# Product operands from host layouts, 1/rms on the results, wider products and some low halves by transfer in a decoder layer

## The chip, the core and the metric

The kernel runs on one core of a Trainium2 chip. The metric is the device time of one execution in microseconds (us). TensorE (PE) multiplies matrices; VectorE (DVE), ScalarE (ACT) and GpSimd (POOL) work on tiles; SyncE (SP) issues the transfers between HBM and the on-chip memory SBUF. Products are summed in PSUM banks of 128 x 512 floats.

## What is computed

The layer takes x of 512 tokens by 1024 features. Everything is float32.

```python
n = rmsnorm(x, norm1_gain)                       # x * rsqrt(mean(x*x) + eps) * gain
q, k, v, u, gates = split(n @ w_in)              # 1024, 1024, 1024, 512, 2048 columns
q, k = rope(rmsnorm(q, q_gain)), rope(rmsnorm(k, k_gain))     # per half head of 64
A = diff_attention(q, k, v, lam)                 # 8 heads, causal; softmax_0 - lam * softmax_1
S = s5_layer(u, ...)                             # a linear recurrence over the tokens, then a GLU
h = x + (sigmoid(g_A) * (A @ w_attn_proj) + sigmoid(g_B) * (S @ w_ssm_proj)) @ w_out
y = h + conv_ffn(rmsnorm(h))                     # w_up, a width-3 causal convolution, a gate, w_down
```

## The kernel before

**Three products for one.** Every float32 operand of a large product is made of a rounded high half and a low half, the rest. `mm3` adds hi·hi, lo·hi and hi·lo into one PSUM bank, so each product of the layer is three matmuls. The activations' halves are `xh`, `xl` (of the normed x, transposed, features on the partitions), `oh`, `ol` (attention), `mh`, `ml` (the mix) and `hh`, `hl` (the second norm).

**Weights.** `load_raw` loads 512 KB into one of 3 buffers `wr`. `split_w` makes the halves: ACT copies `wr` to `wh` (4 buffers, rounded), DVE subtracts to give `wl` (4 buffers). A loaded buffer is free for the next load when both are done.

**Order.** No engine's order is that of the code. The class `Schedule` records every operation with a modelled duration, ranks it by the longest chain behind it plus a number per phase (`sch.boost`), and a list scheduler puts the operations of every engine, SP's transfers too, in a fixed order, within limits on live tiles per class (`sch.caps`). All operations are emitted from one line, L436, so that the profile's groups are told apart by their tiles. The boosts, limits and modelled costs are tables of numbers that decide the order and compute nothing.

**Stages.** (1) The rows of x are loaded; `norm1` squares them on ACT, takes the power -1/2 on POOL (`nrs`), multiplies by 1/rms and gain on DVE (`s_N`), transposes 32 blocks on PE, and writes `xh`, `xl`. (2) q and k of the first head pair (`qk_pair`, by `tok_pair`: 256 columns of weights for two token tiles that share a bank), u (`u_all`, 512 wide, result `Z`), the gates of the S5 branch (`gate_group`, phase `gS`, kept in SBUF), v of the first pair (`v_group`, 256 wide). (3) Four S5 chunks (`s5_const`, `s5_chunk`): constants are built by POOL (`s_T`) and DVE (`k`) from tables of the decay (`dtxe`, `mgxe`), then a scan on DVE with tiles `s_S`; PE transposes and multiplies small float32 blocks between DVE's steps. (4) Projections of the other pairs, the GLU, the S5 projection, eight attention heads, the other gates, the mix, w_out (`tok_pair`, 256 wide), the transposes of `feat`, the second norm, the feed-forward (`ffn`, `down`). Stages overlap: while DVE works on a chunk, PE is given large products.

The widths of a product that the prediction speaks of are the columns that one matmul streams: 256 in `tok_pair`, 512 elsewhere.

Of the kernel before, what the change touches and what calls it, by code (L numbers as in the profile page):

```python
# [15 lines left out]
P = 128  # L16
# [23 lines left out]
C_MASK = 0  # L40
C_DELTA = C_MASK + SEQ
C_COS = C_DELTA + 16
C_SIN = C_COS + NT * HD
C_W = C_SIN + NT * HD

NSLOT = 43


def shape_constants():
    c = np.zeros((P, P + C_W), np.float32)  # L50
    c[:, 0:P] = np.eye(P, dtype=np.float32)
    k = c[:, P:]
    r = np.arange(P)
    k[:, C_MASK + SEQ - P:C_MASK + SEQ] = np.where(r[None, :] <= r[:, None], 0.0, -1e30)
    k[:, C_DELTA:C_DELTA + 16] = (r[:, None] % 16) == np.arange(16)[None, :]
# [3 lines left out]
    cos = np.cos(ang).astype(np.float32)  # L59
    sin = np.sin(ang).astype(np.float32)  # L60
    cc = np.concatenate([cos, cos], -1).reshape(NT, P, HD).transpose(1, 0, 2)
    ss = np.concatenate([-sin, sin], -1).reshape(NT, P, HD).transpose(1, 0, 2)
    k[:, C_COS:C_COS + NT * HD] = cc.reshape(P, -1)
    k[:, C_SIN:C_SIN + NT * HD] = ss.reshape(P, -1)
    return c
# [16 lines left out]
class Op:  # L82
    __slots__ = ("lock", "eng", "calls", "cost", "preds", "succs", "tiles", "alloc", "prio", "npred", "ready", "idx", "start",
                 "end", "nbytes", "phase", "tail", "left", "sim")


class Schedule:
# [4 lines left out]
    DMA_BW = 355.0  # L92
    COLD = 16500.0
# [62 lines left out]
    def _init(self, o, eng):  # L156
        o.eng, o.calls, o.cost, o.preds, o.succs, o.tiles, o.alloc = eng, [], 0.0, {}, [], set(), []
        o.nbytes = 0
        o.lock = False
        o.phase = self.phase  # L160
        o.idx = len(self.ops)
# [102 lines left out]
    def price(self, eng, fn, out, ins, acc, o):  # L264
# [3 lines left out]
        if eng == "PE":  # L268
            if fn == "transpose":
                return 109.0  # L270
            if ins[-1].dtype == F32R:
                c = max(0.4167 * n + 13.5, 98.0 if tuple(ins[0].ap)[-1][0] == 1 else 246.0)

                return c if ins[0].shape[0] > 64 else c / 2
            return 1.667 * n + 11 if out.shape[0] > 32 else 55.0
# [19 lines left out]
        if eng == "POOL":  # L295
            if any(v is ALU.pow for v in [o.calls[-1][2].get("op")]):
# [10 lines left out]
    def rank(self):  # L307
# [3 lines left out]
        for o in reversed(self.ops):  # L311
            dur = o.cost + (1900.0 + o.nbytes / self.DMA_BW if o.eng == "SP" else 0.0)
            o.tail = dur + max([s.tail + self.lat(o, s) for s in o.succs], default=0.0)

    def lat(self, a, b):
        if a.eng == "SP":
            return 0.0
        return self.LAT[a.eng].get(b.eng, 130.0)

    def solve(self):  # L320
# [36 lines left out]
        while done < len(ops):  # L357
# [12 lines left out]
            for e in engs:  # L370
# [31 lines left out]
                o.end = now + cost  # L402
                if e == "SP":
# [35 lines left out]
def build(tc, A, out, dbg=None):  # L439
# [11 lines left out]
    def bc(ap, shape):  # L451
# [9 lines left out]

    sch.caps = {"X": 10, "N": 19, "C": 29, "T": 8, "Z": 15, "S": 18, "G2": 23, "sT": 25, "g": 10, "R": 26,
        "rope": 33, "P": 15, "AT": 15, "O": 8, "pmm": 3, "pa": 2, "px": 1, "po": 1, "p5": 4, "pu": 4, "pq": 9, "pb": 7}

    sch.boost = {"": 6384700, "c0": -125100, "c1": -423900, "c2": 861800, "c3": -573000, "down0": 4913100,
# [5 lines left out]
        "s3": 5910300, "ssm": -676100, "swk": 2750200, "swq": -2342100, "tables": 482600, "u": 1182300,  # L471
# [3 lines left out]
    sch.fifo = set(sch.caps) | {"wr", "wh", "wl", "F", "cv", "h", "mS", "hr"}  # L475
    sch.dram = {"hbuf": {}, "sbuf": {}}
# [117 lines left out]
    vrow = slot("C", [1, 6 * HD])
# [838 lines left out]
```

## Time and profile before

| what | us |
|---|---|
| median of 3 runs | 885.79 (883.72 to 886.74) |
| the profiled execution's own time | 883.83 |
| its span in the trace | 882.1 |
| PE busy | 853.6 (97%) |
| DVE busy | 585.9 (66%) |
| ACT busy | 363.8 (41%) |
| POOL busy | 181.9 (21%) |

The engines work side by side and wait for each other by semaphores. A stretch of the span has a busy time for each engine, and PE a mean granted clock as a share of 2.4 GHz; 0.5 is the lower level of 1.2 GHz. Matmuls overlap in the pipe, so a matmul's own duration is longer than the step from one start to the next; the step is what a stream of them costs. "Idle before, releaser" tells for how long an engine waited ahead of an instruction and what ended the wait.

### The profile page before, as it was taken

What the parts mean: (1) busy time and instruction counts of PE and PEld (TensorE: products, weight loads), DVE (VectorE), ACT (ScalarE), POOL (GpSimd) and SP (SyncE); (2) the same over time, 40 slices, a digit from 0 to 9 for tenths busy, and PEclk for the clock granted to TensorE, in tenths of its full rate; (3) what the DMA queues carried; (4) which work ended last, traced back from release to release, by engine and by line L of the source; (5) the groups of instructions that cost most, each with busy time, mean ns of one, the idle gap of its engine ahead of it and who ended that gap; (6) DMA issues with size and microseconds to landing.
All of it is one profiled execution on the core that took longest, in us unless ns stands there. A gap on an engine that the chain in (4) does not pass through costs nothing.

```text
span 882.1 us, 12703 instructions
## 1 busy us (share of the span) xinstructions
PE 853.6 (97%) x4922; PEld 738.9 (84%) x4922; DVE 585.9 (66%) x1129; ACT 363.8 (41%) x703; POOL 181.9 (21%) x169
## 2 busy tenths in 40 slices
PE   5999899989899999999999999999999999999998
PEld 3998679979679989888889988888888888888887
DVE  4668999899995788864444532599877777324322
ACT  5325462643552466654132531464444444213210
POOL 2445686226103304200000000012211111000000
PEclk9999999989999999999999999999999999999999
DMA  9131113113142301228332652433333333322321
GB/s 286 31 117 49 49 48 94 51 49 97 50 137 91 115 17 49 72 71 273 100 100 85 207 171 76 118 95 96 96 96 95 96 98 99 103 69 86 119 84 59
DMA packets 113208, 85.95 MB, mean 97 GB/s; under 512 B 9634, under 2 KB 99322, under 8 KB 113148
## 3 DMA queue, kind: packets, MB, share of 16 engines
q1 hardware_dynamic: 113148, 85.14, 31.6%
q8 instruction: 38, 0.62, 0.3%
q14 instruction: 22, 0.18, 0.1%
HBM read 78.84 MB, written 6.29 MB: 97 GB/s over the span
## 4 chain that ended last, share of the span: by engine, by line
PE 83%; DVE 10%; ACT 3%; issue 2%; DMA 1%; SPq 1%; POOL 0%; DVEq 0%; ACTq 0%
PE pb L436 83%; DVE s_S L436 4%; DVE wl L436 1%; DVE k L436 1%; DVE s_P L436 1%; DMA s_X<-in_x 1%; ACT s_P L436 1%; DMA wr<-in_w_in 1%; DVE s_rope L436 1%; SPq L436 1%; DVE ml L436 1%; ACT s_G L436 0%; ACT k L436 0%; DVE s_G L436 0%; ACT s_g L436 0%
## 5 line engine op out<-in xcount | busy, mean ns | idle before, releaser
L436 ACT CAST wh<-wr 128x1024 fp32r<-128x1024 f32 (+1 forms) x134 | 139.2, 1039 | 330.1 <-PE pb L436 290.6
L436 DVE TENSOR_TENSOR wl<-wr,wh 128x1024 fp32r<-128x1024 f32 (+1 forms) x134 | 172.3, 1290 | 153.0 <-ACT wh L436 152.6
L436 PE MATMUL pb<-hh,wh 128*128 128x512 f32 (+1 forms) x368 | 140.4, 382 | 0.9 <-ACT wh L436 0.9
L436 PE MATMUL pb<-hh,wl 128*128 128x512 f32 (+1 forms) x368 | 139.8, 380 | 0.0
L436 PE MATMUL pb<-hl,wh 128*128 128x512 f32 (+1 forms) x368 | 139.8, 380 | 0.0
L436 PE MATMUL pb<-wh,xh 128*128 128x256 f32 (+1 forms) x416 | 125.7, 302 | 0.0
L436 PE MATMUL pb<-wh,xl 128*128 128x256 f32 (+1 forms) x416 | 122.2, 294 | 0.1
L436 PE MATMUL pb<-wl,xh 128*128 128x256 f32 (+1 forms) x416 | 122.0, 293 | 0.0
L436 POOL TENSOR_TENSOR s_cv<-s_cv,s_cv 128x512 f32<-128x512 f32 x22 | 37.6, 1707 | 263.1 <-DVE s_cv L436 235.9
L436 PEld LDWEIGHTS pb<-wh,xh 128*128 128x128 f32 x416 | 84.3, 203 | 2.9 <-issue 1.0
L436 PEld LDWEIGHTS pb<-wh,xl 128*128 128x128 f32 x416 | 84.3, 203 | 0.7 <-DVE xl L436 0.4
L436 PEld LDWEIGHTS pb<-wl,xh 128*128 128x128 f32 x416 | 84.2, 202 | 0.0
L436 PEld LDWEIGHTS pb<-hh,wh 128*128 128x128 f32 x368 | 69.2, 188 | 14.2 <-ACT wh L436 1.0
L436 PEld LDWEIGHTS pb<-hh,wl 128*128 128x128 f32 x368 | 69.2, 188 | 13.4 <-issue 0.2
L436 PEld LDWEIGHTS pb<-hl,wh 128*128 128x128 f32 x368 | 69.2, 188 | 13.2
L436 PE MATMUL pb<-wh,s_F 128*128 128x512 f32 (+1 forms) x252 | 71.5, 370 | 0.0
L436 DVE SCALAR_TENSOR_TENSOR s_cv<-s_cv,cw,s_cv 128x511 f32<-128x511 f32 (+1 forms) x88 | 67.7, 805 | 0.0
L436 POOL TENSOR_TENSOR s_T<-k 128x256 f32<-128x256 f32 (+1 forms) x48 | 48.8, 1049 | 22.9 <-DVE k L436 22.9
L436 PEld LDWEIGHTS pb<-wh,s_F 128*128 128x128 f32 x252 | 45.4, 188 | 8.6
L436 PE MATMUL pb<-xh,wh 128*128 128x512 f32 x128 | 52.6, 411 | 0.0
L436 ACT ACTIVATE s_P<-s_P,mx,rq 128x128 f32<-128x128 f32 (+3 forms) x64 | 41.3, 649 | 24.1 <-DVE mx L436 24.1
L436 PE MATMUL pb<-xl,wh 128*128 128x512 f32 x128 | 50.1, 392 | 0.0
(207 smaller groups left out, 1632.1 us busy)
## 6 DMA issues: line engine op xcount, KB each, us to landing
wr<-in_w_in SPq DMA_DIRECT2D x44, 512.0 KB
wr<-in_w_up SPq DMA_DIRECT2D x44, 512.0 KB
wr<-in_w_down SPq DMA_DIRECT2D x20, 512.0 KB
wr<-in_w_attn_proj SPq DMA_DIRECT2D x8, 512.0 KB
wr<-in_w_out SPq DMA_DIRECT2D x8, 512.0 KB
s_X<-in_x SPq DMA_DIRECT2D x8, 256.0 KB
wr<-in_w_ssm_proj SPq DMA_DIRECT2D x4, 512.0 KB
sbuf<-s_g SPq DMA_DIRECT2D x8, 256.0 KB
```

The costliest lines, as they stand in the source:

```text
L436: getattr(e, fn)(*a, **k)
```

## The change

**Layouts made by the host.** x is given a second time transposed (`xt`, 128 x 8 x 512), all weights are cut into 132 tiles of 128 x 1024 (`wt`) that are loaded whole, and the small parameters come laid out and replicated (`pa`, `pb`, `pc`, `rope`, `lam`, `bn`). The transposes of parameters and most spreads by PE are gone.

**1/rms on the results.** `xh`, `xl` are made of `xt` times the gain alone, by one ACT and one DVE operation of 128 x 512 for each of 8 blocks. The power of the mean square (`rs1`) and its spread over the partitions (`rms1`, one 512-wide float32 matmul) come later, and every result is multiplied: `Z` by ACT, q and k within their own norm, v in its two halves' operations, the 16 gate blocks by one more DVE operation each (`V.tensor_mul(g, ps, rms1)`).

**The first product** is u, which needs `xt` and `w_in` two blocks at a time (`k_stream`).

**Wider products.** q and k of a pair share a 512-wide product for each token tile (`qk`), v is made for two pairs at once (`v_half`), w_out in two halves of 512. On PE, 1536 matmuls of 256 columns become 768 of 512; the other large products keep their counts. PE's matmuls go from 4806 to 4000 in all.

**Low halves by transfer.** In the phases `gS`, `v0`, `qk0`, `qk1`, 20 weight tiles in all, ACT writes -hi into `wl` and POOL issues a transfer that adds `wr` to it in SBUF. ACT has 20 more operations of 128 x 1024, POOL 20 transfer issues, DVE 20 subtractions fewer.

**Other moves.** Both sets of gates go through HBM (`gbuf`, `abuf`). Eight matmuls of ones open PE's queue. 1/8 of the softmax is in the rope table. `boost`, `caps` and the modelled costs have new numbers.

```diff
+BY_DMA = ("gS", "v0", "qk0", "qk1")
+WARM = 8
...
+    def split_w(raw):
...
         S.copy(hi, raw)
+        if sch.phase in BY_DMA:
+
+            S.mul(lo, raw, -1.0)
+            G.dma_start(lo, raw, accum_op=ALU.add)
+        else:
             V.tensor_sub(lo, raw, hi.bitcast(F32))
...
+    def k_stream(accs, tiles, lhs, order=None):
+
+        n = len(accs)
+        for j, (wh, wl) in enumerate(tiles):
+            last = j == len(tiles) - 1
+            for i, k in [(i, k) for i in range(n) for k in range(2)] if last else [(i, k) for k in range(2) for i in range(n)]:
+                lh, ll = lhs(2 * j + k, i)
+                with sch.group():
+                    mm3(accs[i], lh, ll, wh[:, k, :], wl[:, k, :], j == 0 and k == 0, last and k == 1)
...
+        S.mul(xh[:, k, :], r, g1col[:, k:k + 1])
+        V.scalar_tensor_tensor(xl[:, k, :], r, g1col[:, k:k + 1], xh[:, k, :].bitcast(F32), op0=ALU.mult, op1=ALU.subtract)
...
+    def gates(off, f):
...
             g = slot("g")
-            S.activation(g, ps, AF.Tanh, scale=0.5)
-            res.append(g)
...
+            V.tensor_mul(g, ps, rms1)
+            S.activation(g, g, AF.Tanh, scale=0.5)
+            f(b, g)
...
+        acc = [pbk("pu") for _ in range(NT)]
+        k_stream(acc, load_k("w_in", KB, (QOFF + 256 * g, 256), (KOFF + 256 * g, 256)), x_tok)
...
+    for ch_ in range(2):
+        sch.phase = f"wout{ch_}"
+        acc = [pbk("pu") for _ in range(NT)]
+        k_stream(acc, load_k("w_out", KB, (512 * ch_, 512)), m_tok)
```

**DVE at the start.** `wl` are low halves of weights, `nms` the mean square, `s_N` the normed x, `s_X` rows of x (of `xt` in the changed kernel). DVE's first instructions before:

```order
L436 TENSOR_TENSOR wl_124<-wr_86,wh_123 128x1024
L436 TENSOR_TENSOR wl_126<-wr_87,wh_125 128x1024
L436 TENSOR_SCALAR nms_108<-nss_105 128x1
L436 SCALAR_TENSOR_TENSOR s_N_110<-s_X_82,nrs_109,pb_103 128x512
L436 SCALAR_TENSOR_TENSOR s_N_112<-s_X_83,nrs_109,pb_104 128x512
L436 TENSOR_TENSOR wl_146<-wr_94,wh_145 128x1024
L436 TENSOR_TENSOR xl<-pb_111,xh 128x4x128
L436 TENSOR_TENSOR xl<-pb_113,xh 128x4x128
L436 TENSOR_TENSOR wl_148<-wr_95,wh_147 128x1024
```

and in the changed kernel, where `cpa` holds the gains:

```order
L485 MEMSET ones 128x128
L485 TENSOR_SCALAR cpa<-cpa 128x4
L485 TENSOR_SCALAR cpa<-cpa 128x1
L485 TENSOR_TENSOR wl_85<-wr_83,wh_84 128x1024
L485 TENSOR_TENSOR wl_90<-wr_88,wh_89 128x1024
L485 TENSOR_TENSOR wl_95<-wr_93,wh_94 128x1024
L485 SCALAR_TENSOR_TENSOR xl<-s_X_82,cpa,xh 128x512
L485 SCALAR_TENSOR_TENSOR xl<-s_X_86,cpa,xh 128x512
```

The norm's steps are gone from ahead of the first `xl`, and three weight tiles stand there.

**POOL at the first S5 chunk.** `s_T` are the decay tables that the chunk's matmuls read, `s_rope` is q or k under the rotation, `qrs` and `rq` are norms of q and k. POOL's instructions before, from the last table of the decay (`mgxe`) on:

```order
L436 TENSOR_TENSOR s_rope_196<-s_rope_194,rck 128x512
L436 TENSOR_TENSOR mgxe_167<-ecol,k_161 128x16
L436 TENSOR_TENSOR s_T_288<-k_161 128x256 x2
L436 TENSOR_TENSOR s_T_289<-k_161 128x256 x2
L436 TENSOR_TENSOR s_rope_204<-s_rope_202,rcq 128x512
L436 TENSOR_TENSOR s_T_291<-k_161 128x256 x2
L436 TENSOR_TENSOR s_T_292<-k_161 128x256 x2
L436 TENSOR_TENSOR qrs_211<-qss_209,mhalf 128x8
L436 TENSOR_TENSOR rq_203<-qss_201,mhalf 128x8
L436 TENSOR_TENSOR s_rope_212<-s_rope_210,rck 128x512
L436 TENSOR_SCALAR rq_203<-rq_203 128x8
```

and in the changed kernel, likewise from `mgxe` on:

```order
L485 TENSOR_TENSOR mgxe_149<-ecol,k_144 128x16
L485 DMA wl_161<-wr_159 128x1024
L485 TENSOR_TENSOR rs_123<-nms_124,mhalf 128x4
L485 DMA wl_164<-wr_162 128x1024
L485 DMA wl_167<-wr_165 128x1024
L485 TENSOR_TENSOR s_T_272<-k_144 128x256 x2
L485 TENSOR_TENSOR s_T_273<-k_144 128x256 x2
L485 TENSOR_TENSOR s_T_275<-k_144 128x256
L485 TENSOR_TENSOR s_T_276<-k_144 128x256
L485 TENSOR_TENSOR s_T_275<-k_144 128x256
L485 TENSOR_TENSOR s_T_276<-k_144 128x256
L485 DMA wl_170<-wr_168 128x1024
L485 DMA wl_209<-wr_207 128x1024
```

Transfers of low halves (`DMA wl`) stand between the multiplies of `s_T` where the norms and rotations stood.

**DVE in the second S5 chunk.** DVE's instructions before, around the first steps on that chunk's results (`s_S<-pb`):

```order
L436 TENSOR_TENSOR wl_270<-wr_266,wh_269 128x1024
L436 TENSOR_TENSOR wl_278<-wr_275,wh_277 128x1024
L436 TENSOR_TENSOR s_S_333<-pb_331,k_162 128x512
L436 TENSOR_TENSOR s_S_334<-pb_332,k_162 128x512
L436 TENSOR_TENSOR s_S_335<-pb_332,k_162 128x512
L436 TENSOR_TENSOR s_S_336<-pb_331,k_162 128x512
L436 TENSOR_TENSOR wl_280<-wr_276,wh_279 128x1024
L436 TENSOR_TENSOR s_S_335<-s_S_335,s_S_336 128x512
L436 TENSOR_TENSOR s_S_333<-s_S_333,s_S_334 128x512
L436 SCALAR_TENSOR_TENSOR s_S_336<-s_T_328,s_S_335 128x512
L436 SCALAR_TENSOR_TENSOR s_S_334<-s_T_328,s_S_333 128x512
```

and in the changed kernel in the same chunk:

```order
L485 TENSOR_TENSOR s_S_317<-pb_315,k_145 128x512
L485 TENSOR_TENSOR s_S_318<-pb_316,k_145 128x512
L485 TENSOR_TENSOR s_S_319<-pb_316,k_145 128x512
L485 TENSOR_TENSOR s_S_320<-pb_315,k_145 128x512
L485 TENSOR_TENSOR s_S_317<-s_S_317,s_S_318 128x512
L485 TENSOR_TENSOR s_S_319<-s_S_319,s_S_320 128x512
L485 SCALAR_TENSOR_TENSOR s_S_318<-s_T_312,s_S_317 128x512
L485 SCALAR_TENSOR_TENSOR s_S_320<-s_T_312,s_S_319 128x512
L485 TENSOR_TENSOR s_S_317<-s_S_318,k_145 128x512
L485 TENSOR_SCALAR qrs_181<-qrs_181,rs_123 128x8
L485 TENSOR_TENSOR s_S_318<-s_S_318,k_145 128x512
```

The subtractions of weights are gone from among the chunk's steps. Ahead of the fourth chunk's last transposes DVE has 28 subtractions of weights before and 5 in the changed kernel.

## Rows read from the trace of the kernel before

**Rows 1.** The page: busy time of each engine, and the chain by engine

```profile
PE 853.6 (97%) x4922; PEld 738.9 (84%) x4922; DVE 585.9 (66%) x1129; ACT 363.8 (41%) x703; POOL 181.9 (21%) x169
...
PE 83%; DVE 10%; ACT 3%; issue 2%; DMA 1%; SPq 1%; POOL 0%; DVEq 0%; ACTq 0%
```

**Rows 2.** Stretches: length, busy PE, PEld, DVE, ACT, POOL (count), clock, DMA share, GB/s

```profile
0.00:40.00 40.00, 29.28 (x182) 25.27 (x182) 20.05 (x38) 16.90 (x33) 11.57 (x26) 0.96 0.59 173
40.00:80.00 40.00, 40.00 (x210) 37.99 (x208) 29.31 (x101) 19.05 (x44) 23.29 (x22) 1.00 0.32 93
80.00:240.00 160.00, 146.81 (x1018) 128.91 (x1018) 150.80 (x296) 73.98 (x163) 75.31 (x74) 0.97 0.20 60
240.00:460.00 220.00, 220.00 (x1385) 189.99 (x1383) 147.56 (x394) 102.03 (x252) 33.14 (x26) 1.00 0.33 102
```

**Rows 3.** Two stretches of 20 us in the S5 stage, same columns

```profile
100.00:120.00 20.00, 17.55 (x85) 14.27 (x85) 19.70 (x34) 8.62 (x19) 11.58 (x12) 0.91 0.15 45
...
180.00:200.00 20.00, 18.01 (x139) 17.26 (x140) 17.84 (x32) 9.61 (x19) 2.55 (x2) 0.83 0.17 54
```

**Rows 4.** Stretch of the first 40 us, instructions that touch xh alone, same columns

```profile
0.00:40.00 40.00, 19.87 (x96) 16.71 (x96) 5.33 (x8) 4.42 (x8) 0.96 0.59 173
```

**Rows 5.** Timeline of PE at 20 us: start, length, instruction, idle time before it

```profile
20.46 0.91 PE L436 MATMUL pb<-ident,s_N 128*128 128x128 f32 x4 [4.37 <-DVE s_N L436]
...
21.38 0.41 PE L436 MATMUL pb<-wh,xl 128*128 128x256 f32 x1
21.59 0.41 PE L436 MATMUL pb<-wl,xh 128*128 128x256 f32 x1
```

**Rows 6.** Timeline of PE: first and last of 9 starts (256), 101 starts (512 columns)

```profile
14.50 0.28 PE L436 MATMUL pb<-wh,xh 128*128 128x256 f32 x1
...
15.46 0.28 PE L436 MATMUL pb<-wl,xh 128*128 128x256 f32 x1
...
649.63 0.39 PE L436 MATMUL pb<-hh,wh 128*128 128x512 f32 x1
...
672.30 0.39 PE L436 MATMUL pb<-hh,wl 128*128 128x512 f32 x1
```

**Rows 7.** Groups by shape: count, busy us, mean ns of one, idle time before

```profile
L436 DVE TENSOR_TENSOR wl<-wr,wh 128x1024 fp32r<-128x1024 f32 x130 | 169.6, 1308 | 135.3 <-ACT wh L436 134.8
L436 DVE TENSOR_TENSOR s_S<-pb,k 128x512 f32<-128x512 f32 x16 | 10.1, 678 | 0.2 <-PE pb L436 0.2
L436 DVE SCALAR_TENSOR_TENSOR s_h<-pb,s_h 128x256 f32<-128x256 f32 x16 | 6.2, 418 | 10.9 <-PE pb L436 10.9
L436 ACT CAST wh<-wr 128x1024 fp32r<-128x1024 f32 x130 | 136.7, 1052 | 311.1 <-PE pb L436 271.6 <-issue 23.6 <-DMA wr<-in_w_in 14.6
L436 POOL TENSOR_TENSOR s_T<-k 128x256 f32<-128x256 f32 x32 | 28.1, 906 | 11.9 <-DVE k L436 11.9
L436 POOL TENSOR_TENSOR s_T<-k 128x512 f32<-128x512 f32 x16 | 20.9, 1335 | 10.9 <-DVE k L436 10.9
L436 PE MATMUL pb<-k,s_S 128*128 128x128 f32 x96 | 16.4, 335 | 5.1 <-DVE s_S L436 5.1
```

**Rows 8.** Landing of weights: SP's issues, and ACT's copies that waited for them

```profile
0.72 0.99 SPq L436 DMA_DIRECT2D wr<-in_w_in  x2
...
3.82 0.43 SPq L436 DMA_DIRECT2D wr<-in_w_in  x1
...
4.43 1.04 ACT L436 CAST wh<-wr 128x1024 fp32r<-128x1024 f32 x1 [2.43 <-DMA wr<-in_w_in]
...
9.13 1.05 ACT L436 CAST wh<-wr 128x1024 fp32r<-128x1024 f32 x1 [0.98 <-DMA wr<-in_w_in]
```

**Rows 9.** Transfers of the first 14 us: packets and bytes

```profile
DMA packets 5034, 3.84 MB, mean 274 GB/s; under 512 B 2257, under 2 KB 4449, under 8 KB 5034
```

**Rows 10.** Timeline of POOL: decay tables, then multiplies for the S5 chunks

```profile
42.67 3.35 POOL L436 TENSOR_TENSOR dtxe<-ecol,k 128x16 f32<-128x16 f32 x1 [1.84 <-DVE qss L436]
...
65.05 2.72 POOL L436 TENSOR_TENSOR s_T<-k 128x256 f32<-128x256 f32 x4 [11.94 <-DVE k L436]
...
120.47 11.71 POOL L436 TENSOR_TENSOR s_T<-k 128x256 f32<-128x256 f32 x12
```

More of the change, by code (lines that the diff above doesn't have):

```diff
@@ L618, in spread @@
-    def spread(r):
-        pb = pbk()
-        T.matmul(pb[:, 0:r.shape[-1]], lhsT=onerow, rhs=r, start=True, stop=True)
-        return pb
+    sch.phase = "warm"
+    wm = pbk()
+    with sch.group():
+        for i in range(WARM):
+            T.matmul(wm[:, 0:P], lhsT=ones, rhs=ones, start=True, stop=True)
     def pow_mhalf(dst, src):
@@ L640, in build @@
+    xs4h = xh.rearrange("p k (j s) -> p k s j", s=4)
+    xs4l = xl.rearrange("p k (j s) -> p k s j", s=4)
+    sch.phase = "u"
+    u_acc = [pbk("pu") for _ in range(4)]
+    k_stream(u_acc, u_w, lambda k, s: (xs4h[:, k, s, :], xs4l[:, k, s, :]))
+    sch.phase = "pc"
+    load(pc, A["pc"])
+    sch.phase = "norm1"
+    xss = small([P, NT, 2], "nss", 1)
     for t in range(NT):
[L641 to L642 removed]
         for hf in range(2):
[L644 removed]
@@ new lines, in build, with row_of @@
+            load(r, A["x"][t * P:(t + 1) * P, hf * 512:(hf + 1) * 512])
+            S.activation(slot("N"), r, AF.Square, scale=1.0 / 32.0, accum_out=xss[:, t, hf:hf + 1])
+    rs1 = const([P, NT], "rs1")
+    xms = small([P, NT], "nms", 1)
+    V.scalar_tensor_tensor(xms, xss[:, :, 0], EPS, xss[:, :, 1], op0=ALU.add, op1=ALU.add)
+    pow_mhalf(rs1, xms)
+    def row_of(rs, dst, cls):
+        dg = slot(cls, [P, NT, P])
+        for t in range(NT):
+            V.tensor_scalar(dg[:, t, :], ident, rs[:, t:t + 1], None, op0=ALU.mult)
+        pr = pbk()
+        T.matmul(pr, lhsT=ones, rhs=dg.rearrange("p t n -> p (t n)"), start=True, stop=True)
+        S.copy(dst, pr)
@@ new lines, in build @@
+    rms1 = const([P, SEQ], "rms1")
+    row_of(rs1, rms1, "N")
+    r4 = rms1.rearrange("p (j s) -> p s j", s=4)
+    pb = pbk()
+    with sch.group():
+        for s in range(4):
+            T.matmul(pb[:, s:s + 1], lhsT=r4[0:1, s, :], rhs=ones[0:1, 0:1], start=True, stop=True)
+    rsu = const([P, 4], "rsu")
+    S.copy(rsu, pb[:, 0:4])
+    Z = {}
+    sch.phase = "uz"
+    for qc in range(4):
+        Z[qc] = slot("Z", [P, 8, 4, 16])
+    for s in range(4):
+        pv = u_acc[s].rearrange("p (z q c) -> p z q c", z=4, q=8)
+        for qc in range(4):
+            S.mul(Z[qc][:, :, 3 - s, :], pv[:, qc], rsu[:, s:s + 1])
@@ L1217, in build, with phase, keep @@
         s5_chunk(qc, d0)
-    qkv(1)
-    sch.phase = "glu"
-    glu()
-    sch.phase = "ssm"
-    ssm_proj()
-    sch.phase = "mid"
+    def phase(name, f, *a):
+        sch.phase = name
+        f(*a)
+    def keep(buf):
+        return lambda b, g: load(A[buf][b * P:(b + 1) * P, :], g)
+    phase("qk0", qk, 0)
+    phase("gS", gates, GSOFF, keep("gbuf"))
+    phase("v0", v_half, 0)
+    for qc in range(4):
+        s5(qc)
+    phase("qk1", qk, 1)
+    phase("glu", glu)
+    phase("ssm", ssm_proj)
     oh = big(F32R, "oh")
@@ L1321, in build @@
     pow_mhalf(rs, ms)
-    dg = slot("hj", [P, NT, P])
-    for t in range(NT):
-        V.tensor_scalar(dg[:, t, :], ident, rs[:, t:t + 1], None, op0=ALU.mult)
-    pr = pbk()
-    T.matmul(pr, lhsT=ones, rhs=dg.rearrange("p t n -> p (t n)"), start=True, stop=True)
-    rms2 = slot("hj")
-    S.copy(rms2, pr)
+    rms2 = rms1
+    row_of(rs, rms2, "hj")
     sch.phase = "ffn"
```

588 lines of the change are left out of this document (243 added, 345 removed), and 15 rows, old and new, of the table psum.

## Prediction

> **What bounds the kernel now.** I began with the busy times and the chain: PE is busy for 853.6 of 882.1 us, and 83% of the chain that ended last is PE, 10% DVE [rows 1]. So a microsecond of PE's stream is a microsecond of the kernel wherever PE never waits, and elsewhere the wait decides. The stretches tell where that is: between 40 and 80 us and between 240 and 460 us PE is busy without a break, but in the first 40 us for only 29.28, and between 80 and 240 us, the stage of the S5 chunks, for 146.81 of 160 [rows 2]. In that stage DVE is busy for 150.80 of 160 us, so there DVE is the bound and PE fills in. The stage loses PE time twice: 13.2 us idle, and a mean granted clock of 0.97, which falls to 0.91 and 0.83 in the stretches of 20 us in which PE has idle time [rows 3]. A mean of 0.97 between 1.0 and 0.5 is 6% of 160 us at half pace, which costs 4.8 us. Together 18.0 us of the stage are not work.
>
> The steps in a steady stream are 0.96 us for 8 matmuls of 256 columns, 0.120 us each, and 22.67 us for 100 of 512, 0.227 us each [rows 6]. At the lower clock (1.2 GHz) the 256-wide step is 0.21 us [rows 5].
>
> **1. The head.** Before, the rows of x are normed and transposed before PE has anything to multiply; at 20 us it waits 4.37 us for `s_N` and comes back at half clock [rows 5]. By 40 us it has done 96 matmuls with `xh` [rows 4], which are two of each three, so 144 of 256 columns. After, the first product needs `xt`, one split and weights. What delays it is DVE's order: the low halves of three weight tiles stand ahead of the first `xl`. Transfers moved 3.84 MB in the first 14 us [rows 9]; the first weights, issued at 0.72 us, were used at 4.43 [rows 8], so allowing 2 us of latency the rate is some 0.32 MB per us. Gains and three tiles are 1.7 MB, the first blocks of `xt` another 0.3, so the third tile lands at 7.5 to 8.4 us; one ACT copy (1.05), one DVE subtraction (1.31) [rows 7] and the split (0.68, by the nearest row of 128 x 512) bring PE's first product to about 10.5 us. Bounds: 9 and 13 us. Of the 29.5 us to 40, half pace after the start costs 2.0 (about 4 us at the lower clock, as before at 20 us), the spread of 1/rms 1.0 and small matmuls 0.3. That leaves 26.2 us, 115 matmuls of 512, which stand for 230 of 256. Against 144, or 72 of 512, that is 43.4 x 0.227 = **-9.9 us** (bounds -7.4 to -11.4 by the start).
>
> **2. Wider products.** 1536 matmuls of 256 become 768 of 512. Each pair saves 2 x 0.120 - 0.227 = 0.013 us [rows 6], 768 x 0.013 = **-10.0 us**, all on PE in stretches where it is full or near it. Rounding of the two steps leaves -8 to -11. The Trainium skill speaks against it: "TensorE: Matmul & The Clock Gate", section on back-to-back issue, gives start to start as N/2.4 GHz plus some 2.5 ns, so that a pair would save 2.5 ns, 1.9 us in all. The rows show 0.120 and 0.227, not 0.109 and 0.216, so the trace does not agree with it; that the overhead would then stay per matmul is taken up among the rivals.
>
> **3. Other PE work that goes.** Sixteen small transposes of parameters, each 0.91/4 = 0.23 at half clock, 0.11 at full [rows 5], and one spread of a row of 384, about 0.5: **-2.3 us**. The eight opening matmuls run while PE has nothing else.
>
> **4. The S5 stage.** Ahead of the fourth chunk's end DVE has 5 subtractions of weights instead of 28; 23 x 1.31 = 30.1 us less [rows 7]. The gate multiplies add 8 x 0.68 = 5.4 us by the nearest row (`s_S<-pb,k`, one PSUM operand). 24.7 us net is more than the 18.0 that the stage loses, so I take the whole loss back, **-18.0 us** (bounds 0 and -18.0). ACT's second pass over 20 tiles, 20 x 1.05 = 21 us [rows 7], lies in a stage where ACT is busy for 74 of 160 [rows 2].
>
> What is late next, three places:
> - *The first chunk's tables.* From `dtxe` to the first multiply of `s_T` before took 65.05 - 42.67 = 22.4 us [rows 10]. After, `dtxe` waits for constants behind some 6.3 MB, at 20 us, so the tables come at 41 to 43 us. PE reaches them after 123 instructions, at about 10.5 + 2.0 + 1.3 + 119 x 0.227 = 40.8. **+2** (bounds 0 and +3).
> - *POOL's queue.* A transfer that makes a low half stands behind POOL's multiplies. Ahead of the eighth (`wl_224`), from the first `s_T` on, are 24 of 256 columns (0.906), 9 of 512 (1.335), 2 of `s_S` (about 1.7) and 4 issues (about 0.9): 40.7 us [rows 7]. From 37 to 40 us that is 78 to 81, and PE wants the tile at about 82. How long the transfer takes no row shows. From below, a load of the same 512 KB with an empty queue took 3.7 us; from above, twice a load with others under way, 5.3 us, is 10.6, since it reads two operands [rows 8]. I take 5, near the lower row, as after the head the transfer engines are busy for 0.2 to 0.3 [rows 2]. It lands between 82 and 86: **+2** (bounds 0 and +10). By the Trainium skill, "DMA: Bandwidth & Descriptors", section on the anatomy of a GpSimd DMA, 2.0 us plus bytes / 436e3 gives 3.2 us, and this term would be 0 to 2; no run here shows that path.
> - *The end of w_out.* Four feature blocks instead of two wait for its last sums; two more splits on two halves, 4 x 0.42 [rows 7]: **+2** (bounds 0 and +3).
>
> **The sum.** -9.9 - 10.0 - 2.3 - 18.0 + 2 + 2 + 2 = -34.2 us. Against the profiled execution's own 883.83 that is 849.6. Its own time lies 2 us under the median of the runs, which is within their spread; I forecast **850**. Edits at nothing: the gates' way through HBM (2 x 2 MB out and back, needed late, while the transfer engines are busy for 0.2 to 0.3 [rows 2]), the softmax's scale in the table (one small DVE operand less), the squares' scale (within an ACT operation that is there already).
>
> **Rivals.**
> - *B, the stage's loss stays.* PE waits in the S5 stage for POOL's tables and transfers or for the chunk's own chain instead of for DVE's queue. For it: the chunk's steps alternate between PE, DVE and POOL, POOL waited 11.94 us for `k` there [rows 10], and its queue now holds transfers that themselves wait for ACT. Against: in that stage POOL was busy for 75 of 160 us, DVE for 151. Without the -18.0 the sum is **868** (862 to 875).
> - *C, slower: the transfers set the pace.* Three `wr` buffers are held until a transfer ends. A tile's cycle is load 3.7, two ACT passes 2.1, its wait W in POOL's queue, issue 0.9, transfer at the upper bound 10.6: 17.3 + W, a third of that per tile. PE spends 24 x 0.227 = 5.45 on a tile, and between the 20 tiles some 232 small matmuls of 0.17 [rows 7], 2.0 per tile: 7.4. To eat the 34.2 us, each of 20 tiles must come 1.7 later, at 9.1, so it decides from W = 10 us. A run of twelve multiplies held POOL for 11.71 us [rows 10]; with W = 12 the pace is 9.8, 20 x 2.4 = 47 us later: **897**. Against it: such runs are few, and the transfer's price is the bound's upper end.
> - *D, the widening gives little.* If what a 256-wide step costs beyond half of a 512-wide one belongs to this stretch of the trace and not to the width, the pair saves next to nothing, and the sum without its -10.0 is **860**. Against it speak the two steady rows [rows 6]. It is where the Trainium skill ("TensorE: Matmul & The Clock Gate", back-to-back issue) would lead, with 858 by its own figure.
>
> **How the numbers follow.** Chances: forecast, 838 to 858, 0.63; B 0.20; C 0.09; D alone 0.08. The range must leave out no more than 2 in 10: from 838 (an early start, no late places: 883.8 - 11.4 - 11 - 2.3 - 18.0 = 841, with 3 for what I can't see) to 870 (D, and most of B); outside are C, the slower part of B and a little below. Faster by over 0.3% (2.65 us, about what a measurement of this kernel can tell from no change) is the forecast, B and D less a little: 0.88; slower by over 0.3% is C, 0.09; the rest 0.03.
>
> **What would show it.** Step 1: PE's first product near 10.5 us, and by 40 us 77 matmuls of 512 with `xh` as one of the operands on either side (two of three of 115). Step 2: 512-wide steps of 0.227 in the products of q, k, v and w_out. Step 4: in the stretch of the S5 chunks a PE that is busy but for a few us at a granted clock of 0.99 or more, and a DVE with waits of its own; POOL's transfers landing 4 to 6 us after their issue. Wrong would make it: idle time of PE put down to POOL or a transfer in tens of us (B, C), or a DVE still full between 40 and 200 us because the work it was relieved of only moved to after the chunks.

## The result, and the profile after

The changed kernel takes 858.13 us (median of 4 runs, 857.12 to 859.43) where the kernel before, on the same chip, takes 884.75. The ratio is 0.970, with a 95% interval of 0.967 to 0.973: 3% faster, 26.6 us. Forecast were 850 and a range of 838 to 870. The profiled execution has a span of 855.4 us against 882.1, 26.7 us less. So the sign and most of the size were as forecast, and 7 to 8 us of the forecast gain are missing.

The page of the changed kernel: busy time by engine, the chain, and two of the transfers (count, KB, median us from issue to landing).

```profile
PE 836.7 (98%) x4126; PEld 689.6 (81%) x4126; DVE 582.6 (68%) x1126; ACT 377.0 (44%) x693; POOL 179.6 (21%) x171
...
PE 88%; DVE 5%; ACT 3%; issue 2%; DMA 1%; POOL 0%; SPq 0%; DVEq 0%; ACTq 0%
...
wr<-in_wt SPq DMA_DIRECT2D x132, 512.0 KB, 3.3
wl<-wr POOLq DMA_DIRECT2D x20, 512.0 KB, 5.4
```

DVE's part of the chain went from 10% [rows 1] to 5%. A transfer that makes a low half lands 5.4 us after its issue (the median of 20); the prediction took 5, between 3.7 and 10.6.

Stretches of the changed kernel (columns as in [rows 2]):

```profile
0.00:40.00 40.00, 33.29 (x132) 30.75 (x133) 23.76 (x96) 26.70 (x48) 16.34 (x27) 0.91 0.89 281
40.00:80.00 40.00, 38.58 (x209) 31.78 (x208) 31.32 (x62) 21.89 (x41) 31.64 (x39) 1.00 0.53 140
80.00:160.00 80.00, 75.43 (x445) 63.42 (x444) 68.27 (x101) 44.53 (x76) 43.22 (x49) 0.98 0.73 186
160.00:240.00 80.00, 79.67 (x409) 63.49 (x409) 71.44 (x167) 37.77 (x88) 19.84 (x13) 1.00 0.34 110
240.00:460.00 220.00, 218.87 (x1105) 173.93 (x1103) 160.56 (x424) 104.69 (x259) 31.77 (x23) 1.00 0.34 116
460.00:600.00 140.00, 139.18 (x671) 116.85 (x672) 92.04 (x122) 60.52 (x90) 13.02 (x9) 1.00 0.37 125
```

The S5 stage now lies between 40 and 200 us. From 40 to 240 PE is idle for 1.42 + 4.57 + 0.33 = 6.3 us, and one stretch of 20 us has a lower clock:

```profile
80.00:100.00 20.00, 17.52 (x100) 14.62 (x99) 15.11 (x19) 10.06 (x18) 10.04 (x12) 0.91 0.72 184
```

A clock of 0.91 is 18% of 20 us at half pace, which costs 1.8 us. The stage loses 6.3 + 1.8 = 8.1 us where it lost 18.0 [rows 2, 3]. DVE, full before, has waits of its own, as forecast, and yet PE still waits for it.

The head, by PE's timeline (start, length, instruction, idle time before), and the count of matmuls that read `xh` in the first 40 us:

```profile
9.64 0.81 PE L485 MATMUL pb<-wh,xh 128*128 128x512 f32 x1 [5.17 <-ACT xh L485]
10.94 0.81 PE L485 MATMUL pb<-wh,xl 128*128 128x512 f32 x1 [0.49 <-DVE xl L485]
...
14.39 0.39 PE L485 MATMUL pb<-wh,xh 128*128 128x512 f32 x1
...
25.67 0.39 PE L485 MATMUL pb<-wh,xh 128*128 128x512 f32 x1
...
37.17 2.02 PE L485 MATMUL pb<-ones,rms 1*128 1x1 f32 x8
```

```profile
0.00:40.00 40.00, 24.32 (x71) 19.18 (x71) 5.38 (x8) 5.40 (x8) 0.91 0.89 281
```

The first product waits for its low half until 10.94 us (forecast 10.5). Half pace ends at about 14.3: the steps from one start to the next go from 0.43 to 0.235 us there. By 40 us there are 71 matmuls with `xh`, two of each three, which stand for 106.5 matmuls, where 77 of 115 were forecast.

### The profile page after: what moved, and what is told of

Read it like the earlier page. It is cut to its first block, busy times and chain, and to the rows that moved or that the text cites. A ratio compares the mean times of both kernels' runs of the same rounds, so it can differ in the third digit from the quotient of the medians.

```text
span 855.4 us, 11173 instructions
## 1 busy us (share of the span) xinstructions
PE 836.7 (98%) x4126; PEld 689.6 (81%) x4126; DVE 582.6 (68%) x1126; ACT 377.0 (44%) x693; POOL 179.6 (21%) x171
## 4 chain that ended last, share of the span: by engine, by line
PE 88%; DVE 5%; ACT 3%; issue 2%; DMA 1%; POOL 0%; SPq 0%; DVEq 0%; ACTq 0%
PE pb L485 88%; DVE s_S L485 1%; DVE k L485 1%; DVE wl L485 1%; DMA wr<-in_wt 1%; DMA wl<-wr 1%; ACT s_Z L485 0%; ACT wh L485 0%; ACT k L485 0%; POOL s_S L485 0%; ACT s_P L485 0%; DVE s_g L485 0%; ACT s_G L485 0%; DVE s_G L485 0%; DVE s_h L485 0%
## 5 line engine op out<-in xcount | busy, mean ns | idle before, releaser
L485 ACT CAST wh<-wr 128x1024 fp32r<-128x1024 f32 x132 | 138.4, 1051 | 247.8 <-PE pb L485 230.9
L485 DVE TENSOR_TENSOR wl<-wr,wh 128x1024 fp32r<-128x1024 f32 x112 | 146.5, 1312 | 143.1 <-ACT wh L485 142.9
L485 PE MATMUL pb<-wh,xh 128*128 128x512 f32 x224 | 92.5, 413 | 5.2 <-ACT xh L485 5.2
L485 PE MATMUL pb<-wh,xl 128*128 128x512 f32 x224 | 88.6, 396 | 0.5 <-DVE xl L485 0.5
L485 PE MATMUL pb<-wl,xh 128*128 128x512 f32 x224 | 88.3, 394 | 0.0
L485 DVE SCALAR_TENSOR_TENSOR s_cv<-s_cv,cpa,s_cv 128x511 f32<-128x511 f32 (+1 forms) x88 | 67.4, 801 | 0.1
L485 PEld LDWEIGHTS pb<-wh,xh 128*128 128x128 f32 x224 | 46.1, 206 | 15.9 <-ACT xh L485 5.4
L485 PEld LDWEIGHTS pb<-wl,xh 128*128 128x128 f32 x224 | 46.0, 206 | 8.1
L485 PEld LDWEIGHTS pb<-wh,xl 128*128 128x128 f32 x224 | 46.1, 206 | 7.5 <-DVE xl L485 1.0
L485 PE MATMUL pb<-xh,wl 128*128 128x512 f32 x128 | 50.2, 392 | 0.6 <-DMA wl<-wr 0.6
```

The lines of the kernel that those rows point to most:

```text
L485: getattr(e, fn)(*a, **k)
```

## The experiments

All are made from the changed kernel and keep its order on every engine but for what the edit says. The cuts of code tell in short what an edit comes to; `...` stands for lines left out. The table has medians and ratios to the kernel before on the same chip; the changed kernel was run once more beside the last runs with pauses.

| kernel | us | ratio, 95% interval |
|---|---|---|
| changed | 858.13 | 0.970 (0.967 to 0.973) |
| changed, again | 860.16 | 0.975 (0.972 to 0.978) |
| low halves on DVE | 865.79 | 0.980 (0.978 to 0.982) |
| 256-wide again | 865.03 | 0.980 (0.977 to 0.983) |
| no multiply of the S5 gates | 857.05 | 0.970 (0.969 to 0.972) |
| x transposed first | 860.12 | 0.973 (0.972 to 0.975) |
| no opening matmuls | 858.35 | 0.971 (0.968 to 0.974) |
| 26 more transfers | 922.35 | 1.043 (1.041 to 1.045) |
| two sums on POOL | 867.91 | 0.981 (0.979 to 0.983) |
| x first, sums on POOL | 861.02 | 0.975 (0.971 to 0.978) |
| pauses on POOL | 861.04 | 0.975 (0.973 to 0.977) |
| x first, pauses on POOL | 859.49 | 0.973 (0.971 to 0.976) |
| tables on DVE | 854.73 | 0.966 (0.964 to 0.968) |

The changed kernel's two medians lie 2 us apart and its two ratios 0.005, which is 4 us. A difference of that size between two kernels is, by itself, not told apart from the spread of one.

### What the transfers and the wider products are worth

```diff
-            S.mul(lo, raw, -1.0)
-            G.dma_start(lo, raw, accum_op=ALU.add)
+            V.tensor_sub(lo, raw, hi.bitcast(F32))   # when ACT's copy has ended
```

> The changed kernel in its own order, but the 20 low halves that it makes by transfer are made by DVE again (20 subtractions of 128x1024, put where ACT's copies have ended; ACT's second pass and POOL's transfer issues are gone). Theory: DVE is the bound of the S5 stage, and the relief is what gave PE's time back there. DVE's busy time between 40 and 200 us rises by about 20 x 1.3 = 26 us, to where it is full, PE's idle time in that stage grows by 10 to 18 us, and the kernel takes 868 to 876 us. Rival: the gain of the stage came from the wider products and the host's layouts, DVE has room for 26 us more among its waits, and the time stays within 3 us of 858.

It took 865.79 us, 5.6 to 7.7 more than the changed kernel's two medians: neither the 10 to 18 of the theory nor nothing. Its stretch from 40 to 80 us and PE's timeline there show where (before `s_S`, DVE's queue):

```profile
40.00:80.00 40.00, 35.65 (x177) 29.46 (x178) 34.52 (x62) 15.30 (x34) 26.00 (x28) 0.89 0.16 53
```

```profile
65.27 3.43 DVE L495 TENSOR_TENSOR wl<-wr,wh 128x1024 fp32r<-128x1024 f32 x2
...
77.15 1.22 PE L495 MATMUL pb<-k,s_S 128*128 128x128 f32 x4 [2.96 <-DVE s_S L495]
```

Two subtractions of weights stand between two steps of a chunk, and PE waits for `s_S`. The clock of the stretch falls to 0.89 (1.00 in the changed kernel), but not by these waits alone: it is 0.62 from 40 to 44.5 us, right behind the eight passes of one column and ahead of the chunk's steps, which costs 1.7 us. So the transfers do what the prediction says, by the mechanism that it names, but 20 subtractions, 26 us by their lengths, bring 4 to 8 us and not 18. DVE's busy time grows by only 19.9 us, from 582.6 to 602.5.

```diff
-    T.matmul(ps, lhsT=lh, rhs=rh, ...)           # and the two others, 512 columns
+    for h in (0, 256):                           # the three of the left half, then of the right
+        T.matmul(ps[:, h:h + 256], lhsT=lh, rhs=rh[:, h:h + 256], ...)
```

> The changed kernel in its own order, but each 512-wide matmul of q, k, v and w_out is issued as two of 256 columns, first the three of the left half, then the three of the right: 768 more matmuls, nothing else. Theory, by the steady steps of 0.120 and 0.227 us: each pair costs 0.013 us more, 768 x 0.013 = 10.0 us, so 868 us, less what lies in places where PE waits anyway (7 to 10 us more than 858). Rival, a fixed part of some nanoseconds for each matmul: 2 us more, 860.

It took 865.03, 4.9 to 6.9 more by the medians; the profiled spans are 864.1 against 855.4 and 857.4 in the changed kernel's two. The steps can be read in the same product, w_out: first and last of 96 starts here, then of 48 in the changed kernel.

```profile
448.82 0.28 PE L489 MATMUL pb<-wh,mh 128*128 128x256 f32 x1
...
460.21 0.28 PE L489 MATMUL pb<-wl,mh 128*128 128x256 f32 x1
```

```profile
442.11 0.39 PE L485 MATMUL pb<-wh,mh 128*128 128x512 f32 x1
...
452.77 0.39 PE L485 MATMUL pb<-wl,mh 128*128 128x512 f32 x1
```

They are 11.39 / 95 = 0.120 us and 10.66 / 47 = 0.227 us, the steps of [rows 6], and PE's busy time is 846.3 us against 836.7 and 838.0. So the width is worth 8 to 10 us of PE's time, and the rival's 2 us falls. Why the medians show less, 5 to 7, was not tried.

### What still ends PE's waits in the S5 stage

```diff
-            V.tensor_mul(g, ps, rms1)
-            S.activation(g, g, AF.Tanh, scale=0.5)
+            S.activation(g, ps, AF.Tanh, scale=0.5)     # the S5 branch's gates alone
```

> The changed kernel in its own order, without the eight multiplies by 1/rms on DVE of the S5 branch's gates (tanh reads PSUM directly), so the gates of that branch are not normed. Theory: DVE's queue still ends PE's waits in the S5 stage, so 8 x 0.68 = 5.4 us less on DVE give 2 to 5 us, 853 to 856. Rival: what is left of the waits there is the chain of a chunk through PE, DVE and POOL, in which these multiplies don't stand; 857 to 859.

857.05: this kernel leaves out the 1/rms of these gates, and the eight multiplies cost nothing that can be told. The amount of DVE's work, less 5.4 us, does not end what is left of the waits, and the theory behind -18.0, that PE's loss follows DVE's load, does not hold for the rest of the loss.

```diff
-   SP: w0 w1 w2 xt0 xt1 ...    ACT: w0 w1 w2 xt0 xt1    DVE: w0 w1 w2 xt0 xt1
+   SP: w0 xt0 xt1 w1 w2 ...    ACT: w0 xt0 xt1 w1 w2    DVE: w0 xt0 xt1 w1 w2
```

> The changed kernel in its own order, but the first two blocks of x transposed are loaded right behind the first weight tile, and their high and low halves are made ahead of the second and third weight tile's. Theory: PE's first product waits for the three weight tiles that stand ahead of the first low half on DVE; it then starts at about 7.5 instead of 9.6 us (waited for low half 8 instead of 10.9), and the kernel takes 2 to 3 us less, 855 to 856. Rival: the transfers then bring the later weights late and PE waits in the stream of u for as long, 858.

860.12, no gain, but not for the rival's reason. PE started at 7.55 us, 2.1 earlier, and half pace ended at the same time, about 14.3; at 35 us some 1.1 us of the start were still won (the same matmul at 34.2 us instead of 35.3). Two things then took it back. Right behind the eight passes of one column, where the changed kernel kept its clock, PE ran at the lower level for over 3 us:

```profile
38.00:41.50 3.50, 3.50 (x10) 2.70 (x11) 2.93 (x9) 3.32 (x14) 3.50 (x6) 0.54 0.98 308
```

That is about 1.6 us lost. And, on DVE, PE and POOL:

```profile
62.40 11.10 DVE L491 TENSOR_TENSOR s_T<-s_T,s_T 128x256 f32<-128x256 f32 x1
...
74.76 3.55 PE L491 MATMUL pb<-k,s_S 128*128 128x128 f32 x16 [3.24 <-DVE s_S L491]
...
62.30 1.61 POOL L491 TENSOR_TENSOR s_S<-s_S,k 128x512 f32<-128x512 f32 x1
63.60 0.89 POOL L491 TENSOR_TENSOR s_T<-k 128x256 f32<-128x256 f32 x1
64.18 1.55 POOL L491 TENSOR_TENSOR s_S<-s_S,k 128x512 f32<-128x512 f32 x1
65.43 7.78 POOL L491 TENSOR_TENSOR s_T<-k 128x256 f32<-128x256 f32 x10
```

A sum of 128x256, 0.41 us elsewhere, takes 11.10 us on DVE and ends when POOL's run of 13 SBUF multiplies ends. The chunk's next step stands behind it, and PE waits 3.24 us for that. This turned the question round: the changed kernel has such rows too. Its DVE and POOL at 107 us:

```profile
108.19 6.82 DVE L485 TENSOR_TENSOR s_T<-s_T,s_T 128x256 f32<-128x256 f32 x1
114.93 0.41 DVE L485 TENSOR_TENSOR s_rope<-s_rope,ropeS 128x256 f32<-128x256 f32 x1
...
107.23 1.50 POOL L485 TENSOR_TENSOR s_T<-k 128x256 f32<-128x256 f32 x2
108.65 1.30 POOL L485 TENSOR_TENSOR s_rope<-s_rope,ropeC 128x512 f32<-128x512 f32 x1
109.88 4.83 POOL L485 TENSOR_TENSOR s_T<-k 128x256 f32<-128x256 f32 x6
114.77 0.88 POOL L485 DMA_DIRECT2D wl<-wr  x1
```

The sum ends when POOL turns from multiplies to a transfer's issue. Another pair of DVE instructions (`k<-s_T,s_T`, 0.68 each elsewhere) takes 4.44 us at 81.31, beside three multiplies of POOL from 81.81 on. PE's two largest waits of the stage, 1.5 us for `k` at 87.6 and 1.8 for `s_S` at 120.9, follow them. The new theory: a DVE instruction that reads two SBUF operands is held for as long as POOL runs one SBUF multiply after another.

As a rule for every run of multiplies this goes too far, by the same trace. From 62.91 to 76.92 us POOL runs 13 SBUF multiplies without a break, and DVE's sums come through between them:

```profile
63.32 1.52 DVE L485 TENSOR_TENSOR s_T<-s_T,s_T 128x256 f32<-128x256 f32 x1
...
65.80 2.81 DVE L485 TENSOR_TENSOR s_S<-s_S,s_S 128x508 f32<-128x508 f32 x2
...
68.53 1.28 DVE L485 TENSOR_TENSOR s_T<-s_T,s_T 128x256 f32<-128x256 f32 x1
...
66.99 9.93 POOL L485 TENSOR_TENSOR s_T<-k 128x256 f32<-128x256 f32 x10
```

Each is longer by about one multiply of POOL (0.99 us each here, 0.78 beside the sum of 11.10 us). The kernel before shows this alone: none of its DVE instructions is longer than the shortest of its form by over 1.2 us. So an instruction is held for a whole run in some places and for one multiply in others, and no run here shows what decides it.

```diff
-        V.tensor_sub(gv[:, 0], ma[:, 0], mb[:, 0])     # and the other sum, chunks 2 to 4
+        G.tensor_sub(gv[:, 0], ma[:, 0], mb[:, 0])
```

> The changed kernel in its own order, but the two sums of 128x256 that join the products of a chunk's first table (s_T from s_T and s_T) are made by POOL instead of DVE in the second to fourth chunk. Theory: such a sum on DVE took 6.82 us at 108 us instead of 0.41, as long as POOL ran one SBUF multiply after another, and PE's wait of 1.8 us at 118.6 for DVE's s_S came of it; without it the wait is gone or under 0.5 us and the kernel takes 855.5 to 857.5. Rival: the DVE instruction is long because of its own operands, or the next instruction with two SBUF inputs is held in its place: 858, with a long DVE instruction elsewhere beside the same POOL run.

867.91, slower, by the rival's second half: the next instruction with two SBUF operands is held in the sum's place. DVE, and PE's waits between 40 and 240 us:

```profile
64.14 14.06 DVE L486 TENSOR_TENSOR s_S<-s_S,k 128x512 f32<-128x512 f32 x2
...
PE pb L486 <- DVE s_S L486: 7.9, 2, 5.0
```

Now it is a step of the chunk itself, two in 14.06 us (the second alone 13.37, beside 16 POOL instructions), and PE waits 5.0 us for it. (Here too the clock is 0.62 from 40 to 44.5 us, 1.7 us lost.) That the victim changes and the length follows POOL's run speaks against the instruction's own operands.

> Both: the first two blocks of x transposed ahead of the second and third weight tile, and the sums on POOL. Theory: the earlier start did save PE 1.3 us up to 40 us and lost it, with 3 us more, at 71 us, where PE waited 3.2 us for a chunk step that stood on DVE behind a sum of 11.10 us beside a POOL run from 62.3 to 73.2; with the sum on POOL the wait goes and the kernel takes 854 to 857. Rival: the chunk's chain from the constants on is fixed in time, and PE waits there for as long whatever comes before: 858 to 860.

861.02 (860.53 to 866.94). The hold at 62 us was not there in its profile, and PE was busy for 38.51 us of 40 between 40 and 80. Instead `k<-s_T,s_T` (two in 4.42 us) and a rotation (8.67 us) were held, and PE waited 4.1 us for `k` up to 88.0 us. So the wait at 71 us went, as the theory has it, and the time did not follow, since other holds took its place.

```diff
   POOL: G.tensor_mul(...)                 # each multiply of the S5 tables
+        G.memset(pause, 0.0)              # 128 x 1
```

> The changed kernel in its own order, with a memset of one element per partition on POOL behind each of its 48 multiplies for the S5 tables. Theory: a DVE instruction with two SBUF inputs that meets an unbroken run of POOL's SBUF multiplies is held until the run ends (6.82, 3.75 and 2.60 us instead of 0.41 to 0.68 in the changed kernel, 13.37 us beside a run of 15 us in the last call), and a short POOL instruction that reads no SBUF lets it in between. Then no such DVE instruction takes over 2 us, PE's waits of 1.5 us at 86 and 1.8 at 118.6 shrink, and the kernel takes 854 to 857. Rival: the runs go on as if unbroken and the holds stay, or POOL, 5 us longer and now waiting for DVE, makes the tables late; 858 to 862.

> The same with the first two blocks of x transposed ahead of the second and third weight tile. Theory: the hold of 11.10 us at 62.4 that ate the earlier start goes, and the start of 2 us earlier shows: 1 to 2 us less than with the pauses alone, 852 to 856. Rival: as without the pauses, 860.

861.04 and 859.49. The pauses let nothing in: the sum at 110 us took 7.04 us, as long as without them. A memset of 0.09 us between two multiplies is no gap. With the earlier start, where no hold at 62 us met it, the median is 1.5 us less than with the pauses alone and 0.7 less than the changed kernel's on the same chip (860.16). The runs of the three overlap, so what the start is worth can't be told.

> The changed kernel itself once more, beside the two others on the same chip: 857 to 860, and in its trace the same held DVE instructions at about 82, 103 and 108 us if the holds hang on the order alone, others or none if they hang on how DVE and POOL happen to meet.

860.16, and in its profile the same three long instructions (6.83, 4.43 and 2.58 us) at 110, 82 and 105. The hold at 62 to 65 us is another matter: it stands in the profile without the opening matmuls (11.5 us), whose DVE and POOL orders are those of the changed kernel, and not in the changed kernel's two. So there it hangs on how the two engines happen to meet, and not on the order alone; what in their meeting decides it is not shown.

The last one takes POOL's runs away:

```diff
-        G.tensor_mul(ma[:, 0], br, pr)      # 48 multiplies of four chunks
+        V.tensor_mul(ma[:, 0], br, pr)
```

> The changed kernel in its own order, but the 48 multiplies for the S5 tables (32 of 128x256, 16 of 128x512) are made by DVE, each at the place where POOL had it. POOL is left with transfers, norms and rotations there. Theory: DVE lost time to POOL's runs, some 33 us between 40 and 240 us by which its instructions are longer than the shortest of their form; without the runs the long ones (6.8, 4.4 and 2.6 us) are at 0.4 to 0.7, which pays for most of the 24 us that the multiplies cost DVE (32 x 0.41 + 16 x 0.68), and no chunk step waits for POOL's tables: 853 to 857. Rival: DVE is then as full as in the kernel before, and the stage's loss returns: 862 to 868.

854.73 (853.26 to 855.19), ratio 0.966 (0.964 to 0.968): the fastest of all. Its five runs all lie under the changed kernel's eight (857.12 and more), though its ratio's interval still touches that of the changed kernel's first four (0.967 to 0.973). The multiplies by shape on DVE, two stretches, and PE's waits between 40 and 240 us:

```profile
L487 DVE TENSOR_TENSOR s_T<-k 128x256 f32<-128x256 f32 x32 | 15.6, 494 | 0.0
L487 DVE TENSOR_TENSOR s_T<-k 128x512 f32<-128x512 f32 x16 | 10.8, 685 | 0.0
L487 DVE TENSOR_TENSOR s_T<-s_T,s_T 128x256 f32<-128x256 f32 x8 | 3.4, 420 | 0.0
```

```profile
40.00:80.00 40.00, 38.59 (x209) 31.96 (x208) 34.11 (x89) 22.05 (x42) 9.98 (x12) 1.00 0.60 149
80.00:160.00 80.00, 77.67 (x459) 65.40 (x458) 68.43 (x126) 45.92 (x80) 28.67 (x31) 0.98 0.70 181
```

```profile
PE pb L487 <- DVE k L487: 2.1, 3, 1.1
PE pb L487 <- ACT s_S L487: 1.0, 1, 1.0
```

DVE has 26.4 us of instructions more (15.6 + 10.8), and from 40 to 160 us it is busy for 102.5 us against 99.6; over the whole span it is busy for 583.4 us against 582.6. Most of the 26.4 us is paid by time that its instructions were held. Between 40 and 240 us, what they take beyond the shortest of their form adds up to 33.4 us in the changed kernel and to 16.8 here. The eight sums take 0.42 us each, the wait for DVE's `s_S` is gone, and PE is busy for 2.2 us more between 80 and 160. This is the experiment in which the theory's cause is taken away, and DVE's busy time does what the theory says. For PE's time a rival stays: with the tables on DVE no engine waits for POOL's tables either (DVE waited 5.3 us for them in the changed kernel's stage), and no run parts the two.

### The opening matmuls and the clock

> The changed kernel in its own order without the eight opening matmuls of ones. Theory, as predicted: they run while PE has nothing else to do and cost nothing; what they may be worth is the clock: with them PE's first products ran at half clock from 9.64 to about 14.2 us, nine matmuls. If the clock rises a fixed time after PE's first work, it will now rise some 4 us later and about ten more matmuls run at half pace, 2 us more: 860. Rival: the rise hangs on the products alone and the time stays 858 within 1 us.

858.35: no difference. PE's timeline without them:

```profile
9.78 0.82 PE L487 MATMUL pb<-wh,xh 128*128 128x512 f32 x1 [9.78 <-ACT xh L487]
...
16.36 0.63 PE L487 MATMUL pb<-wh,xl 128*128 128x512 f32 x1
...
17.07 0.39 PE L487 MATMUL pb<-wh,xh 128*128 128x512 f32 x1
```

Half pace lasts until about 16.9 us, where the changed kernel's first profile has 14.3. That is not the opening matmuls' doing as far as is shown: the changed kernel's repeat, with them, has half pace until about 16.3.

```profile
15.77 0.63 PE L485 MATMUL pb<-wl,xh 128*128 128x512 f32 x1
...
16.50 0.40 PE L485 MATMUL pb<-wh,xl 128*128 128x512 f32 x1
```

In the other runs with the opening matmuls and the same start of PE, between 9.5 and 10.3 us, the first matmul at full pace starts anywhere from 14.5 to 16.8 us. What they do to the clock is not told by one profile.

### Whether the transfers can set the pace

```diff
-BY_DMA = ("gS", "v0", "qk0", "qk1")
+BY_DMA = ("gS", "v0", "qk0", "qk1", "qk2", "qk3", "v1", "glu", "ssm", "gA")    # 46 tiles
```

> The changed kernel in its own order, with 26 more low halves made by transfer (q and k of pairs 2 and 3, v of the second half, the GLU, the S5 projection, the other gates). Theory: a transfer lands some 5.4 us after its issue, and a tile's cycle through three buffers, load 3.3, two ACT passes 2.1, issue 0.9, transfer 5.4, 11.7 us or 3.9 per tile, is under PE's 5.45 per tile, so the transfers don't set the pace; PE loses some 10 us between 240 and 460 us to waits on DVE, of which a part comes back: 854 to 858. Rival (the prediction's slower case): POOL's queue, which waits for ACT and DVE there, holds the transfers back, and PE waits for low halves: 862 or more.

922.35, slower than the kernel before by 4.3%. The order is still that of the changed kernel. The stretch of the later projections and heads, the landing time, and the waits of PE and POOL between 160 and 560 us:

```profile
240.00:460.00 220.00, 186.72 (x875) 142.67 (x874) 120.20 (x386) 106.71 (x261) 50.98 (x43) 0.89 0.46 119
```

```profile
wl<-wr POOLq DMA_DIRECT2D x46, 512.0 KB, 5.2
...
PE pb L486 <- DMA wl<-wr: 29.9, 10, 5.0
...
POOL wl L486 <- ACT wl L486: 141.8, 19, 26.0
```

The transfers are no slower than in the changed kernel, 5.2 us. What is late is their start: POOL waits 141.8 us for ACT's -hi. ACT has the second pass in an order that was made without it, among the heads' work. PE then waits 29.9 us for low halves in ten waits, and the clock falls to 0.89. The prediction's rival C is real, then, with another price in it: not a dear transfer, but W, POOL's wait.

## Why the prediction was nearly right, point by point

**What bounds the kernel** was read rightly: PE where it is full, DVE's queue in the S5 stage.

**1. The head: -9.9 forecast, about -7.8 measured**, (106.5 - 72) x 0.227. Two terms were too small. The small matmuls, eight passes of one column, took 2.02 us, not 0.3. And u's stream steps by (25.67 - 14.39) / 48 = 0.235 us, so some 90 matmuls cost 0.7 us more. Its stationary operand is read with a stride of four, and a weight load takes 0.31 us there, 0.19 where the step is 0.227; that the stride is the cause was not tried. Besides, 144 matmuls of 256 were counted as 72 of 512, which holds 72 x 0.013 = 0.9 us that the second step counts once more: the working's own error. The start (10.94 for 10.5) and half pace (until 14.3) were as forecast, half pace with some luck: it lasts 2 us longer in the repeat.

**2. Wider products: -10.0 forecast**; undone, they cost 5 to 7 us by the medians and 8 to 10 of PE's busy time. The Trainium skill's 1.9 ("TensorE: Matmul & The Clock Gate", section on back-to-back issue) does not agree with that; the steps of 0.120 and 0.227 us do.

**3. Other PE work, -2.3**, was not tested by itself, and no run undoes the host's layouts or 1/rms on the results.

**4. The S5 stage: -18.0 + 2 + 2 forecast, 18.0 - 8.1 = -9.9 measured.** The step that failed is "24.7 us net is more than the 18.0 that the stage loses, so I take the whole loss back". It took DVE's busy time for work. A held instruction counts as busy, and the holds are not relieved by taking subtractions away. From 40 to 240 us, DVE's instructions take 33.0 us beyond the shortest of their form in the kernel before and 33.4 in the changed one. DVE has 18 subtractions fewer there, 23.6 us, yet its busy time falls only from 180.1 us [rows 2] to 171.0. The two late places were sized too high: PE waited 0.85 us for the first chunk's `k` up to 47.4 us (forecast +2), and once, for 0.6 us, for a transfer, the fifth. The eighth (forecast +2) was issued at 81.2 us and landed at 85.7, inside the forecast, and PE did not wait for it. The tables on DVE took 3.4 to 5.4 us off the medians, and 2.0 to 4.0 off the profiled spans (853.4 against 855.4 and 857.4). PE is then idle in the stage for 4.1 us instead of 6.3; waits of 2.1 us for `k` and 1.0 for ACT's `s_S` are left.

**5. The end of w_out: +2 forecast**; PE waits 0.29 us there for `hl`, and its stretch has 139.18 of 140 us.

**Not foreseen**: from 240 to 460 us PE was full before and has 1.1 us idle now. What ends these waits was not tried.

The pieces are -7.8 + 0.9 - 10.0 - 2.3 - 9.9 + 0.3 + 1.1 = -27.7, for 26.7 measured in the spans. The -10.0 and the -2.3 among them are forecasts; with 8 to 10 for the first the pieces come to 26 to 28. Of the rivals, B (the stage's loss stays) came in by half, with a cause that it named in part: POOL, but by its multiplies, not its transfers. C did not come: POOL waited 20.6 us in the stage for ACT's -hi, and PE 0.6 us for a transfer. D fell, by the steps.

## What to carry to other kernels

Before an engine's busy time is taken for work, compare its instructions of one form: those that last many times the shortest may be waiting, and here taking other work off the engine did not bring that time back. A helper engine that holds up the bound one can be worth less than nothing; here 42 us of POOL's multiplies (23.1 + 18.9 by shape) cost DVE most of the 26.4 us that it needs for them itself. Work moved to transfers can start only when the engines ahead of the transfer get round to it: 26 transfers put into an order made without them cost 62 to 64 us. Whether an order made with them in would pay was not tried.

## What the runs showed of the hardware that was not expected

A DVE instruction with two SBUF operands was held in some places by POOL's SBUF multiplies for a whole run of them: 6.82 us beside 9 instructions, 11.10 beside 13, 14.06 for two in the longest, instead of 0.41 to 0.68 each. Memsets of 0.09 us between the multiplies did not let it in; the sum of 6.82 us ended as POOL turned to a transfer's issue. Elsewhere, as from 62.9 to 76.9 us, such instructions came through between the multiplies, each about one multiply late. The Trainium skill ("SBUF — State Buffer", section "SBUF: two separate sides") has it that the one of the two that comes second is blocked until the first one's instruction is over. The rows where DVE comes through one multiply late agree with that; the long holds go further, since there it stays blocked over the instructions that follow.

In the head the clock rose at different times in profiles whose PE had done the same: at about 14.3 us in the changed kernel and 16.3 in its repeat, with the opening matmuls from 1.05 us on and the first product at 9.64 and 10.02 us in these two. With the first product at 6.9 to 7.6 us it rose between 11.5 and 14.5. Behind the eight passes of one column at 36 to 40 us it fell to the lower level for some 3 us in four profiles (low halves on DVE, x first, two sums on POOL, no opening matmuls; 0.51 to 0.54 over 3.5 us) and stayed at 1.00 in the changed kernel's two. None of these differences was tried by itself.
